# A two-layer hybrid trunk on one core: the loads of the first projection all in one queue, and five narrow products of zeros in place of three wide ones

## The chip, the core and the metric

The kernel runs on one core of a Trainium2 chip. A core has a matrix engine (TensorE, PE in the profile; its loads of stationary operands are listed apart as PEld), a vector engine (VectorE, DVE), a scalar engine (ScalarE, ACT), a general engine (GpSimd, POOL) and a sync engine (SyncE, SP). Each takes its instructions in a fixed order and waits on semaphores for the others. Transfers from device memory are issued by SP, ACT or POOL, and the same 16 DMA engines carry them all out. The metric is the device time of one execution, in microseconds (us), as the median of several.

## The reference, cut to what matters

The input x has 512 tokens of 1024 features. Two layers follow each other; each has a token mixer and a gated feed-forward network, both behind an RMS norm and added to the stream. Mixer A is attention over three dilated windows with 8 heads each, mixer B a causal pooling over 2, 4, 8 and 16 tokens. A last RMS norm ends it. All is float32.

```python
def rmsnorm(x, g):
    xf = x.astype(jnp.float32)
    y = xf * lax.rsqrt(jnp.mean(xf * xf, axis=-1, keepdims=True) + RMS_EPS)
    return (y * g.astype(jnp.float32)).astype(x.dtype)
...
for i in range(DEPTH):
    j = i // N_MIXERS
    if i % N_MIXERS == 0:
        x = x + dilated_attention_mixer(rmsnorm(x, attn_norm[j]), w_qkv[j], w_attn_out[j])
    else:
        x = x + pooling_mixer(rmsnorm(x, pool_norm[j]), w_pool_in[j], w_pool_group[j], pool_scale[j])
    x = x + swiglu_ffn(rmsnorm(x, ffn_norm[i]), w_ffn_gate_up[i], w_ffn_down[i])
return rmsnorm(x, final_norm)
```

What matters here is the very first step: the norm of x by `attn_norm`, and the first columns of its product with `w_qkv`.

## The kernel before, in words

**Layout.** The stream is kept transposed, features on the 128 partitions and the 512 tokens along the free dimension, as eight tiles X[0] to X[7] (256 KB each). A weight matrix comes in tiles of 128 by 1024.

**Precision.** A float32 value is kept as two parts, hi (rounded) and lo (what is left). `Product.add` (L234) forms, for each block k of 128 features, three matmuls that add up in one PSUM bank: L245 (hi of the weights with hi of the data), L246 (hi of the weights with lo of the data) and L248 (lo of the weights with hi of the data). The helper `split` (L77) makes the parts of a weight tile: L78 on ACT writes hi, L79 on DVE writes lo. From the second head on, most products use a scheme of seven products in place of eight (`seven`, L393).

**Weights later on.** After the start, `pump` (L165) walks a list of units: it issues a load on SP (L114 and L134 to L137) when a buffer of its ring is free, and splits a loaded unit some units ahead of its use. A ring for raw tiles has four buffers, one for split tiles five.

**The start, lines 698 to 733.** This is the code that the change touches. The norm weights of all norms come in one small tile `nrm` (24 KB), X[0] to X[7] in eight transfers, and the weights of the first four products in eight chunks `w_first[k]` (256 KB each; chunk k holds the block k of all four products). Three issuing engines share these loads:

- ACT's queue: nrm (L698), then X[0] (L700);
- POOL's queue: X[1] to X[7] (L700), then the identity `ident` (L701) and two tables of distances `d0` and `d12` (L702, L703);
- SP's queue: `w_first[0]` to `w_first[7]` (L718).

For each k the kernel then prepares the operands and adds block k to all four products at once:

- the chunk's hi on ACT (L719) and its lo on DVE (L721);
- `scaled` (L286): X[k] times the norm weight; hi on ACT (L292), for k=0 on DVE (L290), and lo on DVE (L293). The factor 1/rms, a number of each token, is multiplied in only after the product;
- `square` (L276): the squares of X[k] on ACT (L278) and their running sum on DVE (L283), from which 1/rms comes (`rstd`, L303: L309 on PE, L312 on DVE, L314 on POOL; `spread`, L317: L322 on PE).

That is twelve matmuls of 512 columns for a k, 96 for the four products. A fifth product follows (L726), the first one whose weights come by `pump` (w_qk, L114), then `rstd`, a sixth product and the rest of the first head.

**Products of zeros.** Ahead of all this, PE multiplies a tile of zeros: DVE fills `idle` (L707), and L710 runs WARM = 3 float32 products of 128 by 128 with 512 columns into a PSUM bank that nobody reads. Each such float32 product stands in the profile as two matmuls.

**What sets the order.** The program is written through a framework that inserts the semaphores and lays out the instructions of each engine by a planner with costs of its own, so that the order on an engine need not be the order of the code. DMAs of one kind share a small set of semaphores in turn; a DMA can therefore wait at its issue for an earlier one to land.

Of the kernel before, what the change touches and what calls it, by code (L numbers as in the profile page):

```python
# [8 lines left out]
F32 = mybir.dt.float32  # L9
# [7 lines left out]
P = 128  # L17
S = 512
D = 1024
KC = D // P  # L20
# [13 lines left out]
H2 = S // 2  # L34
K2 = KC // 2
NPLAIN = 6
WARM = 3
NSOLO = 3
DOWN = (6, 5)
BUFS = {"w": 5, "half": 2, "raw": 4, "rawhalf": 2}  # L40
# [8 lines left out]
def trunk(ctx: ExitStack, tc: tile.TileContext, xT, norms, w_first, w_qk, w_qkp, w_v0, w_v12, w_out, w_pair, w_down, w_pin, w_pgrp,  # L49
          dist0, dist12, ident_in, invcnt_in, outT):  # L50
    nc = tc.nc
# [6 lines left out]
    def x_tile(k, name="x", dtype=F32):  # L58
        return cpool.tile([P, S], dtype, tag=f"x{k}", name=name)

    X = [x_tile(k) for k in range(KC)]
    nrm = cpool.tile([P, NORMS, KC], F32, name="nrm")
# [4 lines left out]
    def ps():  # L67
        return psum.tile([P, S], F32, tag="ps", name="ps")
# [207 lines left out]
    def square(layer, k, engine=None):  # L276
        sq = tmp.tile([P, S], F32, name="sq")
        nc.scalar.activation(sq, X[k], AF.Square)  # L278
        if layer not in acc:
            acc[layer] = sq  # L280
            return
        new = tmp.tile([P, S], F32, name="acc")
        (engine or nc.vector).tensor_add(new, acc[layer], sq)  # L283
        acc[layer] = new

    def scaled(layer, k, hi, lo, on_dve=False):  # L286

        g = nrm[:, layer, k:k + 1]
        if on_dve:
            nc.vector.tensor_scalar(hi, X[k], g, None, op0=OP.mult)  # L290
        else:
            nc.scalar.activation(hi, X[k], AF.Copy, scale=g)  # L292
        nc.vector.scalar_tensor_tensor(lo, X[k], g, hi.bitcast(F32), op0=OP.mult, op1=OP.subtract)  # L293
        operand[layer, k] = hi, lo
# [159 lines left out]
    with tc.tile_pool(name="opool", bufs=1) as opool:  # L454
        early = opool.tile([P, HEADS, S], F32R, tag="o", name="early")
        with tc.tile_pool(name="apool", bufs=1) as apool:
# [238 lines left out]
                return apool.tile([P, S], F32, tag="scratch", name=name, bufs=3)  # L695


            nc.scalar.dma_start(nrm, norms)  # L698
            for k in range(KC):
                (nc.gpsimd if k else nc.scalar).dma_start(X[k], xT[:, k, :])  # L700
            nc.gpsimd.dma_start(ident, ident_in)  # L701
            nc.gpsimd.dma_start(d0, dist0)  # L702
            nc.gpsimd.dma_start(d12, dist12)  # L703
            lead = [Product(KC, stream(0), w=(None, None)) for i in range(NF)]

            idle = apool.tile([P, S], F32, tag="s0", name="idle")
            nc.vector.memset(idle, 0.0)  # L707
            spare = ps()
            for i in range(WARM):
                nc.tensor.matmul(spare, idle[:, :P], idle, start=True, stop=True)  # L710
            for k in range(KC):
                if k % 2 == 0:
                    rawh, wh = Held("raw"), Held("w")
                    rawh.done()
                    wh.done()
                    raw, (hi, lo) = rawh.t, wh.t
                s = slice(k % 2 * NF * P, (k % 2 + 1) * NF * P)
                nc.sync.dma_start(raw[:, s], w_first[k])  # L718
                nc.scalar.activation(hi[:, s], raw[:, s], AF.Copy)  # L719
                scaled(0, k, *U[k], on_dve=k == 0)  # L720
                nc.vector.tensor_tensor(lo[:, s], raw[:, s], hi[:, s].bitcast(F32), op=OP.subtract)  # L721
                for i, f in enumerate(lead):
                    f.w = (hi, lo)
                    f.add([k], pos=k % 2 * NF + i - k)
                square(0, k)
# [90 lines left out]
    with tc.tile_pool(name="fpool", bufs=2) as fpool:  # L816
# [217 lines left out]
        spare = {}  # L1034
# [67 lines left out]
```

## Time and profile before

| | before |
|---|---|
| median of 3 runs | 1278.92 us (1278.1 to 1279.34) |
| the profiled execution | 1279.44 us |
| its span in the trace | 1277.6 us |
| PE busy | 1262.7 us (99%), 8032 matmuls |
| DVE busy | 867.2 us (68%) |
| ACT busy | 529.7 us (41%) |
| POOL busy | 110.6 us (9%) |
| mean granted clock of TensorE | 0.995 |
| bytes moved by DMA | 163.88 MB, 128 GB/s on the mean |

How to read it: the profile is that of one execution. A row of a timeline gives start, duration, engine, line, operation, the tile written and the tiles read, with a count where several equal instructions are merged; in square brackets stands the idle time of the engine ahead of it and what ended that idle time. Matmuls overlap in a pipeline, so the distance between two starts tells more than a duration. In a table of stretches each engine has its busy time with its number of instructions in parentheses; behind them stand the granted clock of TensorE (PEclk, 1.00 is full speed), the busy share of the DMA engines and GB/s. Before the first record of the granted clock the table shows 1.00.

### The profile page before, as it was taken

What the parts mean: (1) busy time and instruction counts of PE and PEld (TensorE: products, weight loads), DVE (VectorE), ACT (ScalarE), POOL (GpSimd) and SP (SyncE); (2) the same over time, 40 slices, a digit from 0 to 9 for tenths busy, and PEclk for the clock granted to TensorE, in tenths of its full rate; (3) what the DMA queues carried; (4) which work ended last, traced back from release to release, by engine and by line L of the source; (5) the groups of instructions that cost most, each with busy time, mean ns of one, the idle gap of its engine ahead of it and who ended that gap; (6) DMA issues with size and microseconds to landing.
All of it is one profiled execution on the core that took longest, in us unless ns stands there. A gap on an engine that the chain in (4) does not pass through costs nothing.

```text
span 1277.6 us, 20114 instructions
## 1 busy us (share of the span) xinstructions
PE 1262.7 (99%) x8032; PEld 1164.0 (91%) x8032; DVE 867.2 (68%) x1313; ACT 529.7 (41%) x825; POOL 110.6 (9%) x112
## 2 busy tenths in 40 slices
PE   8999999999999999999999999999999999999997
PEld 6989999999999998889989999888788988999986
DVE  6694766568566737588736888558978953788643
ACT  6353444444334525345423554333443532455331
POOL 2101101010110100001001110000300000110000
PEclk9999999999999999999999999999999999999998
DMA  8144546445754723147446774343114645676222
GB/s 290 53 127 89 150 115 151 120 108 161 117 124 116 174 76 116 66 99 173 131 134 157 185 182 129 101 146 116 50 67 114 178 130 132 173 182 172 92 69 66
DMA packets 83006, 163.88 MB, mean 128 GB/s; under 512 B 27440, under 2 KB 29504, under 8 KB 82912
## 3 DMA queue, kind: packets, MB, share of 16 engines
q1 hardware_dynamic: 66496, 130.70, 33.0%
q0 software_dynamic: 14976, 30.55, 13.8%
q10 hardware_dynamic: 1440, 1.34, 0.3%
q8 instruction: 63, 1.03, 0.3%
q14 instruction: 31, 0.25, 0.1%
HBM read 160.40 MB, written 2.16 MB: 127 GB/s over the span
## 4 chain that ended last, share of the span: by engine, by line
PE 80%; issue 10%; DVE 6%; DMA 2%; ACT 1%; POOL 0%; DVEq 0%; SPq 0%; POOLq 0%
PE ps L385 12%; PE ps L386 12%; PE ps L384 12%; PE ps L245 9%; PE ps L246 9%; PE ps L248 9%; PE ps L484 2%; PE ps L485 2%; PE ps L486 2%; DVE wlo L79 1%; PE ps L647 1%; PE ps L510 1%; PE ps L509 1%; PE ps L511 1%; PE ps L573 1%
## 5 line engine op out<-in xcount | busy, mean ns | idle before, releaser
L79 DVE TENSOR_TENSOR wlo<-raw,whi 128x1024 fp32r<-128x1024 f32 (+2 forms) x286 | 327.2, 1147 | 203.4 <-ACT whi L78 201.8
L78 ACT ACTIVATE whi<-raw 128x1024 fp32r<-128x1024 f32 (+2 forms) x286 | 283.7, 998 | 421.7 <-PE ps L246 205.6
L245 PE MATMUL ps<-a,whi 128*128 128x512 f32 (+1 forms) x374 | 141.0, 377 | 0.0
L246 PE MATMUL ps<-a,whi 128*128 128x512 f32 (+1 forms) x374 | 140.9, 377 | 0.0
L248 PE MATMUL ps<-a,wlo 128*128 128x512 f32 (+1 forms) x374 | 140.8, 377 | 0.0
L384 PE MATMUL ps<-tt,whi 128*128 128x256 f32 x384 | 108.7, 283 | 0.0
L385 PE MATMUL ps<-tt,whi 128*128 128x256 f32 x384 | 108.7, 283 | 0.0
L386 PE MATMUL ps<-tt,wlo 128*128 128x256 f32 x384 | 108.7, 283 | 0.0
L248 PEld LDWEIGHTS ps<-a,wlo 128*128 128x128 f32 x374 | 70.4, 188 | 13.0
L246 PEld LDWEIGHTS ps<-a,whi 128*128 128x128 f32 x374 | 70.4, 188 | 12.8
L245 PEld LDWEIGHTS ps<-a,whi 128*128 128x128 f32 x374 | 70.4, 188 | 12.6
L137 POOL DMA_DIRECT2D raw<-w_pair x32 | 38.3, 1197 | 446.4 <-DMA raw<-w_pair 180.7
L384 PEld LDWEIGHTS ps<-tt,whi 128*128 128x128 f32 x384 | 73.7, 192 | 0.0
L385 PEld LDWEIGHTS ps<-tt,whi 128*128 128x128 f32 x384 | 73.7, 192 | 0.0
L386 PEld LDWEIGHTS ps<-tt,wlo 128*128 128x128 f32 x384 | 73.7, 192 | 0.0
L385 PE MATMUL ps<-tb,whi 128*128 128x256 f32 x256 | 72.5, 283 | 0.4 <-DVE tb L79 0.4
L386 PE MATMUL ps<-tb,wlo 128*128 128x256 f32 x256 | 72.4, 283 | 0.0
L384 PE MATMUL ps<-tb,whi 128*128 128x256 f32 x256 | 72.4, 283 | 0.0
L245 PE MATMUL ps<-h,whi 128*128 128x512 f32 x160 | 62.7, 392 | 0.0
L248 PE MATMUL ps<-h,wlo 128*128 128x512 f32 x160 | 62.3, 389 | 0.0
L246 PE MATMUL ps<-h,whi 128*128 128x512 f32 x160 | 62.3, 389 | 0.0
L384 PE MATMUL ps<-h,whi 128*128 128x256 f32 x216 | 61.8, 286 | 0.0
(248 smaller groups left out, 3334.1 us busy)
## 6 DMA issues: line engine op xcount, KB each, us to landing
raw<-w_pair SPq DMA_DIRECT2D x76, 512.0 KB, 4.3
raw<-w_qkp SPq DMA_DIRECT2D x36, 512.0 KB, 4.6
raw<-w_pair POOLq DMA_DIRECT2D x32, 512.0 KB, 6.9
raw<-w_v SPq DMA_DIRECT2D x24, 512.0 KB, 3.3
raw<-w_down SPq DMA_DIRECT2D x32, 384.0 KB, 3.0
raw<-w_down SPq DMA_DIRECT2D x32, 320.0 KB, 2.8
raw<-w_qkp POOLq DMA_DIRECT2D x18, 512.0 KB, 7.1
rawhalf<-w_pair SPq DMA_DIRECT2D x32, 256.0 KB, 3.3
```

What stands on the lines that cost most here:

```text
L78: nc.scalar.activation(hi, v, AF.Copy)
L79: nc.vector.tensor_tensor(lo, v, hi.bitcast(F32), op=OP.subtract)
L137: nc.gpsimd.dma_start(self.b.t.rearrange("p (a c) -> p a c", a=2), self.src[:, None, 3 * S:].to_broadcast([P, 2, S]), accum_op=OP.add)
L245: nc.tensor.matmul(self.p[:, cols], w[0][:, s], mh[:, cols], start=self.done == 0, stop=False)
L246: nc.tensor.matmul(self.p[:, cols], w[0][:, s], ml[:, cols], start=False, stop=False)
L248: nc.tensor.matmul(self.p[:, cols], w[1][:, s], mh[:, cols], start=False, stop=self.done == self.n)
L384: nc.tensor.matmul(dst, w.t[0][:, c], th, start=k == 0, stop=False)
L385: nc.tensor.matmul(dst, w.t[0][:, c], tl, start=False, stop=False)
L386: nc.tensor.matmul(dst, w.t[1][:, c], th, start=False, stop=k == K2 - 1)
L484: nc.tensor.matmul(ps4[b], oph[:, b, :], wh, start=k == 0, stop=False)
L485: nc.tensor.matmul(ps4[b], oph[:, b, :], wl, start=False, stop=False)
L486: nc.tensor.matmul(ps4[b], opl[:, b, :], wh, start=False, stop=k == KC - 1)
```

## The change

The norm weights and the eight X[k] are no longer issued by ACT and POOL. SP issues them: nrm first, and then, inside the loop over k, X[k] right before `w_first[k]`. POOL keeps `ident`, `d0` and `d12`, which are now its first transfers. The number of products of zeros goes from three to five, and each has 256 columns in place of 512; the tile of zeros is half as wide.

```diff
-WARM = 3
+WARM = 5
...
-            nc.scalar.dma_start(nrm, norms)
-            for k in range(KC):
-                (nc.gpsimd if k else nc.scalar).dma_start(X[k], xT[:, k, :])
+            nc.sync.dma_start(nrm, norms)
             nc.gpsimd.dma_start(ident, ident_in)
             nc.gpsimd.dma_start(d0, dist0)
             nc.gpsimd.dma_start(d12, dist12)
             lead = [Product(KC, stream(0), w=(None, None)) for i in range(NF)]

-            idle = apool.tile([P, S], F32, tag="s0", name="idle")
+            idle = apool.tile([P, H2], F32, tag="s0", name="idle")
             nc.vector.memset(idle, 0.0)
             spare = ps()
             for i in range(WARM):
-                nc.tensor.matmul(spare, idle[:, :P], idle, start=True, stop=True)
+                nc.tensor.matmul(spare[:, :H2], idle[:, :P], idle, start=True, stop=True)
             for k in range(KC):
...
                 s = slice(k % 2 * NF * P, (k % 2 + 1) * NF * P)
+                nc.sync.dma_start(X[k], xT[:, k, :])
                 nc.sync.dma_start(raw[:, s], w_first[k])
```

## The prediction

> **What bounds the kernel now.** I read the head of the page first, then the list of what TensorE (PE) waited for, then the first microseconds engine by engine.
>
> ```profile
> span 1277.6 us, 20114 instructions
> PE 1262.7 (99%) x8032; PEld 1164.0 (91%) x8032; DVE 867.2 (68%) x1313; ACT 529.7 (41%) x825; POOL 110.6 (9%) x112
> ```
> ```profile
> PE ps L245 <- DVE early L290: 2.5, 1, 2.5
> PE ps L710 <- DVE idle L707: 1.5, 1, 1.5
> PE ps L322 <- POOL rcol L314: 1.1, 1, 1.1
> ```
>
> PE is the bound: 99% busy, and the columns of the second list (us in total, times, longest) show that two of its largest waits lie at the very start: 1.5 us before its first product and 2.5 us before the first real one. What the change can win must come out of that start; whatever PE does earlier there, the end should follow. Here is PE's start, from its timeline (start, duration, line, count).
>
> ```profile
> 1.50 4.96 PE L710 MATMUL ps<-idle 128*128 128x512 f32 x6 [1.50 <-DVE idle L707]
> 9.01 1.85 PE L245 MATMUL ps<-early,whi 128*128 128x512 f32 x4 [2.54 <-DVE early L290]
> 10.66 0.63 PE L246 MATMUL ps<-early,whi 128*128 128x512 f32 x1
> 11.09 0.63 PE L248 MATMUL ps<-early,wlo 128*128 128x512 f32 x1
> ...
> 13.43 0.39 PE L245 MATMUL ps<-early,whi 128*128 128x512 f32 x1
> ...
> 14.12 0.39 PE L245 MATMUL ps<-early,whi 128*128 128x512 f32 x1
> ```
>
> The pitch is what counts, since durations overlap: 0.43 us (10.66 to 11.09) early, and three matmuls in 0.69 us, 0.23 us each, from 13.43 on. So PE starts its real work at 9.01 and does it at half speed for a while. The granted clock says for how long (the first pair of numbers is the stretch and its length, PEclk the third from the end):
>
> ```profile
> 9.01:9.30 0.29, 0.29 (x1) 0.26 (x2) 0.29 (x1) 0.29 (x2) 0.13 (x1) 0.86 1.03 410
> 9.30:12.50 3.20, 3.20 (x9) 2.45 (x8) 2.88 (x6) 3.20 (x7) 0.41 (x1) 0.50 1.03 386
> 12.50:12.70 0.20, 0.20 (x2) 0.19 (x1) 0.20 (x1) 0.20 (x2) 0.00 (x0) 0.67 0.92 338
> ```
>
> A mean of 0.86 over 0.29 us puts the fall to one half at about 9.22, and 0.67 over 0.20 us puts the return at about 12.63: 3.41 us at half speed, 1.7 us lost. PE thus stands as if it had begun at full speed at 9.01 + 1.7 = **10.7 us**. I call this its effective start.
>
> Why is k=0 so late? The other engines:
>
> ```profile
> 0.96 0.48 DVE L707 MEMSET idle<- 128x512 f32 x1
> 4.28 0.69 DVE L721 TENSOR_TENSOR wlo<-raw,whi 128x512 fp32r<-128x512 f32 x1 [2.83 <-ACT whi L719]
> 7.71 0.75 DVE L293 SCALAR_TENSOR_TENSOR early<-x,nrm,early 128x512 fp32r<-128x512 f32 x1 [2.73 <-ACT early L292]
> 8.38 0.48 DVE L290 TENSOR_SCALAR early<-x,nrm 128x512 fp32r<-128x512 f32 x1
> ```
> ```profile
> 0.72 0.41 ACTq L698 DMA_DIRECT2D nrm<-norms  x1
> 1.23 0.39 ACTq L700 DMA_DIRECT2D x<-xT  x1
> 3.62 0.63 ACT L719 ACTIVATE whi<-raw 128x512 fp32r<-128x512 f32 x1 [0.96 <-DMA raw<-w_first]
> 6.95 0.72 ACT L292 ACTIVATE early<-x,nrm 128x512 fp32r<-128x512 f32 x1 [2.71 <-DMA x<-xT]
> ```
> ```profile
> x<-xT ACTq DMA_DIRECT2D x1, 256.0 KB, 4.0
> ```
>
> The first weights are split by 5.0 and X[0] lands at 1.23 + 4.0 = 5.2. But L290, the only instruction of k=0 that needs X[0] first, stands on VectorE (DVE) behind an L293, which waits for L292 on ScalarE (ACT). An L293 subtracts what L290 or L292 has written; L290 writes for k=0 and comes later here, so this L293 is of k=1 and waits for X[1], which GpSimd (POOL) fetches and which is there at 6.95. The order laid out for DVE took X[1] to come before X[0]. That is 8.38 - 5.2 = 3.2 us of delay made by queues, not by data.
>
> **The change, step by step.**
>
> 1. *Warm-up.* The memset halves: 0.24 us by proportion, 0.48 if its cost is fixed, so PE starts at 1.26 to 1.50; I take 1.27, since far smaller memsets of this kernel are far shorter. The weight loads of the six warm-up matmuls give the pitch:
>
> ```profile
> 4.23 0.34 PEld L710 LDWEIGHTS ps<-idle 128*128 128x128 f32 x1 [0.52 <-issue]
> 5.08 0.34 PEld L710 LDWEIGHTS ps<-idle 128*128 128x128 f32 x1 [0.52 <-issue]
> ```
>
> That is 0.85 us for one of two matmuls of a product of 512 columns. Five products of 256 columns are ten matmuls of 0.43, 4.27 us: they end at **5.5** (5.8 by the longer memset) instead of 6.46.
>
> 2. *Arrival of k=0.* On SP stand nrm, X[0], w_first[0] in this order. The first issue is at 0.73, as now; by the ACT rows the two ahead of the weights take 0.41 and 0.39, so w_first[0] is issued at 1.53.
>
> ```profile
> 0.73 4.60 SPq L718 DMA_DIRECT2D raw<-w_first  x8
> ```
> ```profile
> DMA to landing us min/median/max: 2.9/9.9/12.3
> ```
>
> The fastest w_first, the first one, lands 2.9 us after its issue (0.73 + 2.9 = 3.6, where L719 starts). With the same delay X[0] lands at 4.0 and w_first[0] at 4.4. For the bounds: the bytes that all engines moved are 47, 234 and 389 KB in the three microseconds from 1 on; nrm, X[0] and w_first[0], 549 KB, are in by 3.7 at that rate, which is the lower bound; with the 4.0 of X[0] on ACT's queue the weights land at 5.5, the upper.
>
> ```profile
> 1.00:2.00 1.00, 0.49 (x1) 0.50 (x2) 0.45 (x1) 0.84 (x1) 0.74 (x1) 1.00 0.17 47
> 2.00:3.00 1.00, 1.00 (x2) 0.34 (x2) 0.00 (x0) 0.65 (x2) 1.00 (x3) 1.00 0.69 234
> 3.00:4.00 1.00, 1.00 (x2) 0.34 (x1) 0.00 (x0) 0.38 (x1) 1.00 (x3) 1.00 1.09 389
> ```
>
> I take 4.4, the row nearest in kind. L719 (0.63) then ends at 5.0 and L290 (0.48, from 4.0) at 4.5; L293 ends at 5.2 and L721 at 5.9, needed only after the four L245. So PE could begin at 5.0 (6.2 by the upper bound), inside or just behind the warm-up: real work starts at **5.5**, without a gap.
>
> 3. *The clock.* In the profile the grant changes at 9.22 and 12.63, 3.41 apart. One step earlier is 5.8; a rise there fits the warm-up, whose six pitches of 0.85 would end at 6.6 and not by 6.46 without it. If the steps lie so again, the real work runs at half speed from 5.5 to 5.8, 0.15 us lost: effective start **5.7**. [...]
>
> 4. *Does it stay fed?* PE eats a k in 12 x 0.23 = 2.7 us. DVE, the slower of the two that prepare it, repeats its three instructions of a k every 1.86:
>
> ```profile
> 12.93 0.74 DVE L293 SCALAR_TENSOR_TENSOR early<-x,nrm,early 128x512 fp32r<-128x512 f32 x1
> ...
> 14.79 0.75 DVE L293 SCALAR_TENSOR_TENSOR early<-x,nrm,early 128x512 fp32r<-128x512 f32 x1
> ```
>
> The DMA engines, at the 389 GB/s above, bring a pair (524 KB) in 1.35 us. POOL no longer issues X, so ident, d0 and d12 (393 KB by their shapes) come early and may push the second pair back by up to 1.0 us: it lands by 6.8 at the latest and, with L719 and L721 behind it, is ready at 8.1; PE, done with k=0 after 0.15 + 2.7, wants it at 8.4. That is close, and every later k has 0.9 us more. SP now has 17 issues in a row, 0.57 us each by the L718 row (4.60 for 8), and
>
> ```profile
> SPq L718 <- DMA nrm<-norms: 0.3, 1, 0.3
> ```
>
> shows that a ninth DMA waits for the first to land. With eight in flight, 5 us of transfer, that costs no bandwidth. Behind them on SP stands the first w_qk load, which may move by a microsecond either way. Its user is the fifth product:
>
> ```profile
> 22.64 3.49 DVE L79 TENSOR_TENSOR wlo<-raw,whi 128x1024 fp32r<-128x1024 f32 x3
> ```
>
> The first of these three splits is done at about 23.8. PE reaches it at 10.7 + 96 x 0.23 = 32.6 now and at 27.6 then, so 3.8 us of cover remain even if DVE did not move at all. Later splits wait for PE itself, and move with it.
>
> 5. *The end.* PE's last four small products run at half speed there and at full speed earlier:
>
> ```profile
> 1262.53 0.60 PE L322 MATMUL ps<-ident,rcol 128*128 128x128 f32 x4
> ...
> 1269.62 1.22 PE L322 MATMUL ps<-ident,rcol 128*128 128x128 f32 x4 [1.10 <-POOL rcol L314]
> ```
>
> Shifted against the steps of the clock they may save up to 0.6; I take 0.2.
>
> **Sum.** 10.7 - 5.7 = 5.0 us at the start, 0.2 at the end. The profiled execution took 1279.44 (span 1277.6 and 1.84 around it), 0.5 above the median: 1279.44 - 5.2 = **1274.2 us**.
>
> [...]
>
> **Rivals.**
>
> [...]
>
> *B: k=0 is still late.* DVE or ACT again has a k=1 instruction ahead of one of k=0. X[1], fourth in the queue, has its 262 KB 0.7 us after w_first[0], at 5.1, or at 5.8 beside POOL's loads; L292 (0.72), L293 (0.75) and L290 (0.48) after it end at 7.7. PE pauses 2.2 us. If the clock holds, that is the effective start and the time 1276.2; if it falls as it does now, 1.7 more, 1277.9. For it: just that inversion stands in the present order. Against: X[0] now is ahead of everything but nrm.
>
> *C: the gain is given back.* The fifth product, or a later split, doesn't come sooner and PE waits for it. From 3.8 us late on it costs one for one; 1276.5 to 1278.9. Against: the longest wait of PE after 9.01 is 1.1 us, and that for POOL.
>
> *D: slower.* One mechanism: the single queue feeds PE's first ks too slowly. Now PE begins k=7 at 10.7 + 7 x 2.7 = 29.8. With 2 us of work-up, the last pair must land after 27.8 to make the end later than it is, that is 3.3 us for each pair behind the first at 4.4: the queue would have to fall to 157 GB/s. At 4.0 us a pair PE would begin k=7 at 34.4, 4.6 later than now, and the time would be 1284. For it: the median w_first took 9.9 us to land, by the row above, if beside other queues. Against: the 389 GB/s.
>
> **Chances.** Forecast with A 66%, B 16%, C 12%, D 6%. A difference of under 0.2%, 2.6 us, can hardly be told from none; that puts the border at 1276.4. Faster: 66 + 5 of B + 3 of C = 74%; same: 11 + 9 = 20%; slower: 6%. The range begins at 1272.9 (the earliest rise, 0.6 at the end, and half of the 0.5 by which the profiled execution lies above the median) and reaches to 1277.2, with most of B and the better part of C's low end, which leaves out 20%.
>
> **What would show it.** In the changed profile: L290 ahead of every L293 on DVE, at about 4; L710 as ten matmuls ending near 5.5 to 5.8; the first L245 then, with no wait of over 0.7 us; a granted clock that has no stretch at 0.50 beginning after 9; the fifth product begun near 27.6. An L245 after 7, a half-speed stretch to 12, or new PE waits past 27 would show the forecast wrong.

## The result, and the profile after

The changed kernel takes 1275.68 us (median of 22 executions, 1274.39 to 1278.55) beside 1278.93 us before (22 executions, 1276.94 to 1280.93): a ratio of 0.9977, with an interval of 0.997 to 0.9983. It is 3 us faster; 4.7 had been forecast. The time lies within the predicted range, and the gain came from where it was looked for, the start of PE; two terms of the sum, the landing of the first weights and the rise of the clock, had the wrong size.

The profiled execution of the changed kernel took 1277.5 us, its span is 1275.7. Head of its page, and the list of what PE waited for:

```profile
span 1275.7 us, 20125 instructions
PE 1262.7 (99%) x8036; PEld 1165.3 (91%) x8036; DVE 866.3 (68%) x1313; ACT 529.4 (41%) x825; POOL 106.4 (8%) x105
```
```profile
PE ps L322 <- POOL rcol L314: 1.3, 2, 1.1
PE ps L708 <- DVE idle L705: 1.2, 1, 1.2
PE ps L309 <- ACT sq L1002: 0.8, 1, 0.8
...
PE ps L245 <- ACT whi L718: 0.5, 1, 0.5
```

The wait of 2.5 us for L290 is gone. In its place stands one of 0.5 us for L718, the hi of the first weights (line numbers of this part have moved: L708 is the product of zeros, L718 was L719, L720 was L721). PE's timeline, and then the instructions on DVE and ACT that make k=0 ready:

```profile
1.24 4.63 PE L708 MATMUL ps<-idle 128*128 128x256 f32 x10 [1.24 <-DVE idle L705]
6.41 0.79 PE L245 MATMUL ps<-early,whi 128*128 128x512 f32 x1 [0.54 <-ACT whi L718]
...
9.56 0.63 PE L246 MATMUL ps<-early,whi 128*128 128x512 f32 x1
9.99 0.55 PE L248 MATMUL ps<-early,wlo 128*128 128x512 f32 x1
10.38 0.39 PE L245 MATMUL ps<-early,whi 128*128 128x512 f32 x1
10.61 0.40 PE L246 MATMUL ps<-early,whi 128*128 128x512 f32 x1
```
```profile
4.30 0.49 DVE L290 TENSOR_SCALAR early<-x,nrm 128x512 fp32r<-128x512 f32 x1 [3.12 <-DMA x<-xT]
4.82 0.75 DVE L293 SCALAR_TENSOR_TENSOR early<-x,nrm,early 128x512 fp32r<-128x512 f32 x1
...
5.73 0.63 ACT L718 ACTIVATE whi<-raw 128x512 fp32r<-128x512 f32 x1 [0.89 <-DMA raw<-w_first]
```

Three things are to be seen. L290 now stands ahead of every L293 on DVE and runs at 4.30 in place of 8.38. The first weights land only at 5.73, so real work begins at 6.41, 0.54 us after the zeros. And its pitch is 0.43 us up to 9.99 and 0.23 us from 10.38 on: the clock rises at about 10.3 (the first record of the granted clock is at 10.31), and 3.9 us of real work ran at half speed.

With half of that lost, the effective start is 6.4 + 1.95 = 8.4 us, against 10.7 before: 2.4 us gained at the start. To see what becomes of them, I follow one instruction through both traces: L314 on POOL, which stands once in each norm. First the kernel before (start, duration), then the changed one; the rows at 39.17 and 36.81 are the first norm.

```profile
39.17 1.04 POOL L314 TENSOR_TENSOR rcol<-var,nhalf 128x4 f32<-128x4 f32 x1 [19.83 <-DVE var L312]
...
869.47 1.95 POOL L314 TENSOR_TENSOR rcol<-var,nhalf 128x4 f32<-128x4 f32 x1 [105.12 <-DVE var L312]
928.38 1.02 POOL L314 TENSOR_TENSOR rcol<-var,nhalf 128x4 f32<-128x4 f32 x1 [2.15 <-DVE var L312]
1260.36 0.71 POOL L314 TENSOR_TENSOR rcol<-var,nhalf 128x2 f32<-128x2 f32 x1 [88.41 <-DVE var L312]
```
```profile
36.81 1.04 POOL L314 TENSOR_TENSOR rcol<-var,nhalf 128x4 f32<-128x4 f32 x1 [28.75 <-DVE var L312]
...
867.41 1.95 POOL L314 TENSOR_TENSOR rcol<-var,nhalf 128x4 f32<-128x4 f32 x1 [105.53 <-DVE var L312]
926.32 1.96 POOL L314 TENSOR_TENSOR rcol<-var,nhalf 128x4 f32<-128x4 f32 x1 [2.19 <-DVE var L312]
1258.90 0.71 POOL L314 TENSOR_TENSOR rcol<-var,nhalf 128x2 f32<-128x2 f32 x1 [88.45 <-DVE var L312]
```

The lead is 2.36 us at the first norm, 2.06 at the third and fourth, and 1.46 at the last part of the kernel. The largest step down goes along with an L314 of 1.96 us where the trace before has one of 1.02. PE waits for that L314,

```profile
928.34 1.16 PE L322 MATMUL ps<-ident,rcol 128*128 128x128 f32 x8 [0.20 <-POOL rcol L314]
```

and starts this L322 1.74 us ahead of the trace before (930.08), so about 0.3 us of the 0.6 go there; the rest goes later, and its place is not shown. At the end 0.5 us come back:

```profile
1268.16 0.71 PE L322 MATMUL ps<-ident,rcol 128*128 128x128 f32 x4 [1.10 <-POOL rcol L314]
```

These are the products that took 1.22 us at half speed before. There the granted clock falls to one half at 1268.7 (a mean of 0.74 over the half microsecond from 1268.5), ahead of these products at 1269.62; here it falls at 1269.8 (0.83 over the half microsecond from 1269.5), behind them. In a second execution of the changed kernel (after_again, below) they take 1.19 us.

```profile
1265.99 1.19 PE L322 MATMUL ps<-ident,rcol 128*128 128x128 f32 x4 [1.10 <-POOL rcol L314]
```

So this pair of traces shows 1.9 us in the spans; the medians of 22 executions differ by 3.25, because the executions of one kernel differ among each other by up to 4 us, and at 1277.5 us this execution is among the longer ones of its kernel. Why they differ is the first question for the runs.

### The profile page after: what moved, and what is told of

Its sections match the earlier page's. It is cut to its first block, busy times and chain, and to the rows that moved or that the text cites. A ratio compares the mean times of both kernels' runs of the same rounds, so it can differ in the third digit from the quotient of the medians.

```text
span 1275.7 us, 20125 instructions
## 1 busy us (share of the span) xinstructions
PE 1262.7 (99%) x8036; PEld 1165.3 (91%) x8036; DVE 866.3 (68%) x1313; ACT 529.4 (41%) x825; POOL 106.4 (8%) x105
## 4 chain that ended last, share of the span: by engine, by line
PE 80%; issue 10%; DVE 6%; DMA 2%; ACT 1%; POOL 1%; SPq 0%; DVEq 0%; POOLq 0%; ACTq 0%
PE ps L385 12%; PE ps L384 12%; PE ps L386 12%; PE ps L245 9%; PE ps L248 9%; PE ps L246 9%; PE ps L484 2%; PE ps L485 2%; PE ps L486 2%; DVE wlo L79 2%; PE ps L647 1%; PE ps L510 1%; PE ps L509 1%; PE ps L511 1%; PE ps L573 1%
```

## The experiments

My theory after the result: the time is set by the effective start of PE, which is made of (1) when the operands of k=0 are ready and (2) when the clock rises, and the rise stands at no fixed distance from the start. The rivals: the zeros themselves carry the gain; the single queue as such does; the order of DVE alone does. The table gives, for each run, the median of its executions and of the kernel before on the same chip, the ratio with its interval, and from its profile PE's first real matmul and the start of the L314 of the first norm (39.17 in the profile before), which sums up the effective start. The ratio is not the quotient of the two medians but lies near that of the means (for e3 the medians alone give 0.9978). e4_tables_late, e4_again and e10_x_rows have five executions each, the changed kernel 22, the others eleven or twelve.

| run | us | before | ratio | first real | L314 |
|---|---|---|---|---|---|
| changed kernel | 1275.68 | 1278.93 | 0.9977 (0.9970 to 0.9983) | 6.41 | 36.81 |
| after_again | 1275.91 | 1278.80 | 0.9983 (0.9973 to 0.9994) | 6.35 | 35.22 |
| e1_queue_only | 1276.45 | 1279.69 | 0.9976 (0.9968 to 0.9985) | 6.96 | 35.81 |
| e2_zeros_only | 1279.09 | 1279.69 | 0.9999 (0.9990 to 1.0007) | 8.89 | 40.26 |
| e3_six | 1276.81 | 1279.69 | 0.9993 (0.9981 to 1.0005) | 7.30 | 36.07 |
| e6_eight | 1276.67 | 1278.80 | 0.9985 (0.9976 to 0.9994) | 8.01 | 36.85 |
| e8_none | 1277.67 | 1278.92 | 0.9993 (0.9984 to 1.0001) | 7.49 | 37.63 |
| e5_x0_sp | 1276.77 | 1278.80 | 0.9984 (0.9976 to 0.9993) | 7.16 | 36.15 |
| e9_two_queues | 1276.35 | 1278.80 | 0.9985 (0.9976 to 0.9994) | 6.32 | 36.06 |
| e4_tables_late | 1274.66 | 1279.69 | 0.9967 (0.9954 to 0.9980) | 5.55 | 35.76 |
| e4_again | 1274.41 | 1278.92 | 0.9968 (0.9955 to 0.9980) | 5.56 | 34.83 |
| e10_x_rows | 1274.51 | 1278.92 | 0.9965 (0.9953 to 0.9977) | 5.4 | 33.97 |

### The same kernel again

No edit.

> The changed kernel once more, unaltered, beside the other three on one chip. If the phase of the clock's steps is free, as I hold, the rise in this profile lies at another distance from the start than the 10.3 of the first one; if it is tied to the start, it is 10.3 again within 0.3. Time 1275.7 within 1, the executions spread over 3 us or more.

```profile
6.35 0.57 PE L245 MATMUL ps<-early,whi 128*128 128x512 f32 x1 [0.48 <-ACT whi L718]
6.76 0.39 PE L246 MATMUL ps<-early,whi 128*128 128x512 f32 x1
6.99 0.40 PE L245 MATMUL ps<-early,whi 128*128 128x512 f32 x1
```

Real work starts at 6.35, as in the first profile, and after the zeros the same pause stands, but the pitch is 0.23 us from 6.76 on: the clock rose at about 6.5, not 10.3. The rise is not tied to the start. L314 comes 1.6 us sooner (35.22 for 36.81) with the first real product at nearly the same time, and the execution took 1275.81 in place of 1277.5: this is most of the difference between the two executions. Spread of this set: 1274.8 to 1278.7.

The pause in itself did not hold the clock down here: it lies within the 3.41 us before this rise (the distance of the two changes of the clock in the profile before, 9.22 and 12.63), too.

```profile
3.12:6.53 3.41, 2.93 (x8) 1.83 (x7) 1.44 (x3) 1.26 (x2) 1.20 (x2) 1.00 0.92 309
```

PE was busy for 2.93 us of this stretch, and the clock rose. In the first profile it was busy for 2.88 of the 3.42 us that end at 6.90, and the pitch stayed at 0.43 us. The first profile is the exception: by the clock records of the traces, the rise comes ahead of the first real product, at 4.2 to 7.2 us, in each of the eight profiles below that have products of zeros and L290 ahead of every L293.

### The two parts of the change, each alone

e1_queue_only:

```diff
-WARM = 5
+WARM = 3
...
-            idle = apool.tile([P, H2], F32, tag="s0", name="idle")
+            idle = apool.tile([P, S], F32, tag="s0", name="idle")
...
-                nc.tensor.matmul(spare[:, :H2], idle[:, :P], idle, start=True, stop=True)
+                nc.tensor.matmul(spare, idle[:, :P], idle, start=True, stop=True)
```

> The queue part of the change alone: nrm, X and the first weights on SP as in the changed kernel, but three products of zeros of 512 columns as before. [...] Three wide products end at about 6.6, so there is no pause: PE goes on into the real products at 6.6, the clock rises by 8.3 at the latest, effective start 6.6 to 7.5 against 8.4 in the profile of the changed kernel; time 1274.8 (1273.9 to 1275.7), not slower than the whole change. Rival: the narrow products carry a part of the gain; then this is 1 us or more slower than the whole change, 1276.7 or above.

e2_zeros_only has the same lines the other way round, in the kernel before.

> The zeros part alone: the queues as before, five products of zeros of 256 columns. My theory: k=0 is still ready at about 9.0 us, the zeros end at 5.9, PE pauses 3.1 us, the clock falls or has not risen at all; effective start 10.5 to 11, time 1278.9 within 0.8, no gain. Rival: five narrow products warm the clock better than three wide ones; then 1.5 us faster, 1277.4.

The queue alone gives 0.9976, the whole of the gain (its median of 1276.45 lies above the 1273.9 to 1275.7 expected, on a chip where the kernel before takes 1279.69); the zeros alone give 0.9999. So the new zeros add nothing that these runs can see, with or without the new queue. The profile of e1 departs from its expectation in one point: its weights landed at 6.27, and PE paused after all,

```profile
6.96 0.50 PE L245 MATMUL ps<-early,whi 128*128 128x512 f32 x1 [1.02 <-ACT whi L718]
7.29 0.40 PE L246 MATMUL ps<-early,whi 128*128 128x512 f32 x1
```

but at full clock, and the clock stayed up through the pause of 1.02 us (pitch 0.23 us from 8.03 on). In e2 the other case can be seen, in an execution that was the longest of its set (1281.02). Its clock fell at 8.09, before the real work at 8.89, and this whole stretch then ran at half (PE busy 2.60 us of 3.41, clock 0.50):

```profile
8.09:11.50 3.41, 2.60 (x6) 2.15 (x7) 3.41 (x7) 3.41 (x7) 0.54 (x1) 0.50 1.04 404
```

The clock came back only at about 14.9 (pitch 0.43 us up to 14.58, 0.23 from 14.97 on). That cost its L314 1.1 us against the kernel before.

### More zeros, and none

```diff
-WARM = 5
+WARM = 6
```

> The changed kernel with six products of zeros instead of five. My theory: the zeros end at 6.4 to 6.5, the pause of 0.5 us ahead of the first real product is gone, the clock rises by 8.1 at the latest: effective start 6.5 to 7.4, time 1274.7, 1 us faster than the changed kernel. Rival: a pause of 0.5 us does not matter to the clock, the late rise at 10.3 in that profile was chance; then the time is that of the changed kernel, 1275.7, or 0.1 more.

e6_eight has WARM = 8, e8_none has WARM = 0.

> The changed kernel with eight narrow products of zeros instead of five. [...] Eight products last to 8.1 if the clock does not rise, so there is no pause before it has; effective start 6.9 to 8.1 in every execution. The executions then lie closer together (within 1.5 us, where the changed kernel spreads over 4), and the median is that of the changed kernel within 0.7. Rival: the spread of the changed kernel has nothing to do with the clock at the start; then it stays at 3 us or more, and the median is 0.5 to 1 us higher for the longer zeros.

> The changed kernel without any product of zeros. [...] Rival: the zeros buy nothing once the loads come in order; then the ratio is 0.998 as for the changed kernel.

More zeros buy nothing. Six gave 0.9993, with three of its twelve executions at 1281 to 1283; no trace of one of these was taken, and their cause stays open. Its profile, at 1275.47, shows why the reasoning of "no pause" fell: the clock rose early, at about 4.2, the twelve matmuls of zeros ended at 5.5 where the ten of the changed kernel ended at 5.87, and PE paused 1.78 us until the weights had come:

```profile
7.30 0.50 PE L245 MATMUL ps<-early,whi 128*128 128x512 f32 x1 [1.78 <-ACT whi L718]
```
```profile
4.17:7.58 3.41, 1.63 (x7) 1.13 (x7) 1.53 (x3) 1.46 (x3) 2.23 (x3) 1.00 1.01 337
```

So a number of zeros was no fixed time in these two profiles. And after the pause the clock was still up (pitch 0.23 us from 7.64 on), with 1.63 us of work in the 3.41 us shown. Eight zeros did not narrow the spread to 1.5 us (1275.3 to 1279.3), so the clock at the start is not its only source: the landing of the first weights varies too, from 5.7 to 7.3 us in the six profiles in which SP brings all of X and POOL's tables are its first transfers (the changed kernel twice, e1, e3, e6, e8).

None at all gave 0.9993, where I had expected 0.9992 (0.9985 to 1.0), an estimate with real work at half speed for 3 to 6.5 us: 1.3 to 2.0 us worse than the changed kernel by the ratios. Its interval lies just above that of the changed kernel's first set and overlaps that of after_again, so this is likely, not shown. The missing zeros are not all that the profile shows: the weights landed at 6.80 and real work began at 7.49, not at 6.41 as in the changed kernel, so a part of its late L314 is the landing and not the missing zeros. Its first matmuls, cold, and the first warm ones:

```profile
7.49 0.79 PE L245 MATMUL ps<-early,whi 128*128 128x512 f32 x1 [7.49 <-ACT whi L718]
8.08 0.63 PE L246 MATMUL ps<-early,whi 128*128 128x512 f32 x1
8.50 0.63 PE L248 MATMUL ps<-early,wlo 128*128 128x512 f32 x1
...
10.97 0.39 PE L248 MATMUL ps<-early,wlo 128*128 128x512 f32 x1
11.21 0.40 PE L245 MATMUL ps<-early,whi 128*128 128x512 f32 x1
```

The pitch is 0.43 until 10.6 and 0.23 from 10.97 on: 3.4 us ran at half speed, 1.7 us lost. It is the one trace without zeros.

### POOL's tables out of the way

```diff
             nc.sync.dma_start(nrm, norms)
-            nc.gpsimd.dma_start(ident, ident_in)
-            nc.gpsimd.dma_start(d0, dist0)
-            nc.gpsimd.dma_start(d12, dist12)
...
                 square(0, k)
+            nc.sync.dma_start(d0, dist0)
+            nc.sync.dma_start(d12, dist12)
+            nc.sync.dma_start(ident, ident_in)
             lead += begin(1, 0, range(KC))
```

> The changed kernel, but ident, d0 and d12 go through SP's queue behind the last first weight, so POOL issues none of the first transfers. My theory: POOL's three transfers are what delays w_first[0] (landed at 5.7 where 4.4 was forecast); without them it lands by 4.8, PE begins right behind the zeros at 5.9, effective start 5.9 to 7.0, time 1274.2. Rival: the low rate of 132 GB/s between 3 and 4 us has another cause (the latency of the queue's first transfers); then w_first[0] lands at 5.4 or later and the time is that of the changed kernel within 0.5.

> The run with the late tables once more, unaltered: ident, d0 and d12 on SP behind the last first weight, five narrow products of zeros. My theory: without POOL's transfers among the first ones w_first[0] lands at 4.9 in place of 5.7, PE goes on from the zeros at 5.6 without a pause, so 1 us or more is gained on the changed kernel: ratio to the kernel before 0.9972 or less. The pause of 1.06 us at k=1 in the first profile of this kernel was one DMA engine that came 2.8 us behind the other fifteen; it is chance and need not be there again. Rival: the five executions of the first time were lucky; then the ratio is that of the changed kernel, 0.998.

This is the term that the prediction had missed. The stretch from 3 to 4 us, first in the changed kernel and then in e4_again (last number: GB/s):

```profile
3.00:4.00 1.00, 1.00 (x4) 0.73 (x4) 0.00 (x0) 0.00 (x0) 0.12 (x1) 1.00 0.59 132
```
```profile
3.00:4.00 1.00, 1.00 (x4) 0.73 (x4) 0.00 (x0) 0.00 (x0) 0.00 (x0) 1.00 0.83 283
```

and what follows on ACT and PE in e4_again:

```profile
4.88 0.63 ACT L715 ACTIVATE whi<-raw 128x512 fp32r<-128x512 f32 x1
```
```profile
5.56 0.50 PE L245 MATMUL ps<-early,whi 128*128 128x512 f32 x1 [0.18 <-ACT whi L715]
5.90 0.39 PE L246 MATMUL ps<-early,whi 128*128 128x512 f32 x1
```

Without POOL's 393 KB beside them the first weights land at 4.88 in place of 5.73, real work starts at 5.56, at full clock, and 4.3 us are gained at L314. The landing differs by more in the other profiles: it is at 4.7 to 4.9 us in the three with late tables and one queue (e4 twice, and e10 below) and at 5.7 to 7.3 in the six named above. All engines together moved less in this microsecond beside POOL's transfers (132 against 283 GB/s), so it is more than the sharing of one rate; why is open. This kernel is very likely also the faster one: 0.9967 and 0.9968 on two chips, 1.2 to 2.0 us below the changed kernel by the ratios (0.9983 and 0.9977 less 0.9968 and 0.9967, of 1279). The two intervals overlap in part with those of the changed kernel, so it is the two agreeing repeats, and e10 with 0.9965, together with the rows above that carry this. In the first profile of this kernel PE paused 1.06 us at k=1, where w_first[1] landed at 8.9; the records of landing show that fifteen of its sixteen shares had come by 6.1 and the last at 8.9. In the second it landed at 7.2.

### Order or queue?

e5_x0_sp moves one transfer of the kernel before:

```diff
-            for k in range(KC):
-                (nc.gpsimd if k else nc.scalar).dma_start(X[k], xT[:, k, :])
+            nc.sync.dma_start(X[0], xT[:, 0, :])
+            for k in range(1, KC):
+                nc.gpsimd.dma_start(X[k], xT[:, k, :])
```

> The kernel before with one transfer moved: X[0] goes out on SP ahead of w_first[0]; nrm stays on ACT, X[1] to X[7] and the tables on POOL, three wide products of zeros. DVE's order laid out for it has L290 first. My theory: most of the gain of the change is that the instruction of k=0 no longer stands behind one of k=1. L290 then runs at about 4.2 and w_first[0] lands at about 5; PE starts its real work at 6.6, right behind the zeros, and waits again for k=1 (X[1] by POOL lands at 6.9, so the second k is ready at about 8.5, no long pause). Effective start 6.8 to 8, time 2.5 us or more below the kernel before: ratio 0.998 or less. Rival: the single queue is what counts, because X[1] to X[7] on POOL hold up the first ks; then the gain is under 1 us, ratio over 0.999.

e9_two_queues is e4 with two words changed:

```diff
-            nc.sync.dma_start(nrm, norms)
+            nc.scalar.dma_start(nrm, norms)
...
-                nc.sync.dma_start(X[k], xT[:, k, :])
+                nc.scalar.dma_start(X[k], xT[:, k, :])
```

> As the run with the late tables (ident, d0, d12 on SP behind the last first weight), but nrm and all X go out on ACT's queue and only w_first on SP. Five narrow products of zeros. The order laid out for DVE has two L717 and L290 ahead of the first L293. My theory: two queues shared by the same DMA engines bring X[k] and w_first[k] side by side, so a pair arrives as with one queue, no later than 5.7; what counted in the change is that POOL does not bring X. PE starts at 5.6 to 6.2, time as with the late tables on one queue, 1274.7 within 0.7. Rival: one queue in the order of need is what counts; on two queues the loads of later ks run ahead of those of k=0, PE starts at 7 or later and the time is 1 us or more above that.

In e5 only X[0] has moved, DVE's order has turned, and L290 runs at 4.17:

```profile
4.17 0.49 DVE L290 TENSOR_SCALAR early<-x,nrm 128x512 fp32r<-128x512 f32 x1 [2.72 <-DMA nrm<-norms]
```

The ratio, 0.9984, lies within the interval of the changed kernel on the same chip (0.9983). So the bulk of the gain comes with moving X[0]; taking X[1] to X[7] off POOL adds less than these runs can tell apart. The move does two things, since X[0] also lands sooner (4.0 in place of 5.2), and a run with the order alone turned was not made. By the rows of the kernel before, an L290 run at 5.2 would have ended at 5.7, ahead of the end of the zeros at 6.46, so the order by itself could account for the wait of 2.5 us; that is an estimate.

On ACT the inversion came back: the first weights, issued at 1.16, landed 3.5 us later (4.7), but their hi stands behind the L292 of k=1.

```profile
5.87 0.72 ACT L292 ACTIVATE early<-x,nrm 128x512 fp32r<-128x512 f32 x1 [1.24 <-DMA x<-xT]
6.50 1.13 ACT L720 ACTIVATE whi<-raw 128x512 fp32r<-128x512 f32 x2
```
```profile
7.16 0.50 PE L245 MATMUL ps<-early,whi 128*128 128x512 f32 x1 [1.34 <-ACT whi L720]
```

So e5 pays for a k=1 instruction ahead of one of k=0 as well, only less.

For e9 my theory fell and the rival held. The two queues are served side by side, w_first[0] lands at 3.56, but X[0] only at 5.7:

```profile
5.68 0.49 DVE L290 TENSOR_SCALAR early<-x,nrm 128x512 fp32r<-128x512 f32 x1 [0.77 <-DMA x<-xT]
```

and PE starts at 6.32, 0.8 us later than with one queue; the time is 0.9985 against 0.9967 and 0.9968 (on other chips). With the tables gone, one queue in the order of need gives about 2 us over two queues by these ratios. DVE's order turned too (an L717 ran at 4.23, ahead of this L290), but it was done at 4.92 and the row names the transfer as what L290 waited for; the ratios are of different chips and their intervals overlap a little, so the 0.8 us at the start is the firmer number. Not all of the 2 us need be the sharing of two queues: ACT also computes, and it issued X[1] only at 3.57, behind an L715,

```profile
3.57 0.34 ACTq L713 DMA_DIRECT2D x<-xT  x1
```

where SP issues it at 2.1 in e4. A second queue on an engine that does not compute was not tried.

### How x lies in memory

e10_x_rows is e4 with x stored as eight contiguous blocks, so that X[k] is read as one (a later load of x, on POOL, is changed in the same way):

```diff
-                nc.sync.dma_start(X[k], xT[:, k, :])
+                nc.sync.dma_start(X[k], xT[k])
...
-        "xT": v["x"].reshape(S, KC, P).transpose(2, 1, 0),
+        "xT": v["x"].reshape(S, KC, P).transpose(1, 2, 0),
```

> As the run with the late tables, but x lies in device memory so that each X[k] is one contiguous block of 256 KB, as each w_first[k] is, in place of 128 rows 16 KB apart. The order of all instructions is the same. Theory: it makes no difference, since the rows of 2 KB are the same transfers; X[0] lands at 4.2 and the time is that of the late tables within 0.7. Rival: the low rate of the first microseconds (132 GB/s between 3 and 4 us in the changed kernel, 285 with the late tables) comes from the stride of x; then X[0] and w_first[0] land 0.5 us sooner or more.

```profile
3.76 0.49 DVE L290 TENSOR_SCALAR early<-x,nrm 128x512 fp32r<-128x512 f32 x1 [2.58 <-DMA x<-xT]
```
```profile
4.72 0.63 ACT L715 ACTIVATE whi<-raw 128x512 fp32r<-128x512 f32 x1 [0.42 <-DMA raw<-w_first]
```

X[0] lands 0.5 us sooner than in e4 (L290 at 3.76 in place of 4.30), the weights 0.15 sooner, and PE has no pause in the first ks. The rival was right on X[0], not on the weights, and the time, 0.9965, cannot be told from e4's.

## Why the prediction was right, and where its sizes were off

**What bounds the kernel**: right. PE's start was the place, and what was won there reached the last norm but for 0.9 us of 2.36 in this pair of traces.

**Step 1, the zeros**: 4.27 us from 1.27 were forecast, ending at 5.5; the last of the ten matmuls ends at 5.87 in the profile, with its tail, from a start at 1.24. Right.

**Step 2, arrival of k=0**: the step that failed. L290 ahead of every L293, with X[0] at 4.0 forecast and 4.2 measured, was right. The landing of w_first[0] was put at 4.4, at the most at 5.5; it was 5.7, beyond the bound. The transfers of ident, d0 and d12 were seen, but step 4 had them start after k=0 was in and push back the second pair. They hit the first: POOL issues them at 1.3 to 3.1 now that nothing stands ahead of them on POOL, while the seven X kept them until 5.2 before. e4 measures the term: 0.85 us of the 1.3 at the landing. The other half microsecond is there without the tables too: in e4_again w_first[0] is issued at 1.63, not 1.53, and lands 3.2 us later (4.88), where the forecast gave the third transfer of a queue the 2.9 us that the first one had taken.

**Step 3, the clock**: the rise 3.41 us before 9.22 was carried over as if tied to the start, with an effective start of 5.7. It is not tied: the clock rose at 10.3 and 6.5 in two profiles of one kernel. The effective start was 8.4 in the first: of the 2.7 us beyond the forecast 0.9 are the later real start, the rest the later rise. The 3.42 us that end 3.41 us before that rise, at 6.9, have a pause of 0.54 us in them; those before the rise in after_again have one of 0.48 us, so a pause alone doesn't explain it. PE was busy for 2.88 us of the one and 2.93 of the other; what decides between them was not shown. No run shows an earliest or a latest rise either, as the range (its "earliest rise"), rival A (8.1) and the expectations of e1, e3 and e6 (8.3 and 8.1) took it: those were estimates of mine, and the rise came at 10.3, at 6.5 and, in e3, at 4.2. With rises this far apart in one kernel, a mean over several profiles would have served the forecast better than the one of the profile before.

Chance has a part in the number 1274.2. e4_again has nearly what the forecast assumed, the landing at 4.9, a pause of 0.18 us and an early rise; by L314 it starts effectively at 10.7 - 4.3 = 6.4, not 5.7, and its profiled execution took 1274.2, the very number forecast, because its lead grew from 4.3 us at the first norm to 5.1 at the last, for reasons not looked into.

**Step 4, fed afterwards**: right. PE's waits after 6.41 are those of before within 0.2 us (the longest, for L314, is again 1.1), and the fifth product moved along with the start, from 32.5 to 30.1 where 27.6 was forecast.

**Step 5, the end**: 0.2 was taken of a bound of 0.6; the profile had 0.5, after_again next to nothing (1.19 against 1.22). It goes by when the clock falls there, at 1268.7 in the profile before and at 1269.8 in the first of the changed kernel.

**The rivals**: A, a rise at 8.1 and a time of 1275.3, is in kind what the first profile shows, with a rise at 10.3. B and D did not occur (D's 29.8 is 29.6 by its own terms, which changes nothing). C, a gain given back, is a part of the first pair of traces: 0.3 us up to the third norm and 0.6 from the fourth on, beside an L314 that took 0.9 us longer. That L314 takes about 2.0 us in every profile with L290 ahead of every L293 (1.96 in both of the changed kernel) and 1.0 us in the two without (the kernel before, 1.02, and e2); what makes it so wasn't tried.

## What to carry to other kernels

When an engine waits at the start, look at what its feeder was made to wait for: here a transfer that had landed at 5.2 was used at 8.38, because the laid-out order put an instruction of the next step ahead of it, and moving one transfer (e5) gave most of the gain. A transfer that is taken off a queue lets the ones behind it start sooner, and here they delayed the most urgent ones; move the tables that nobody needs yet behind them (e4: very likely one to two microseconds more). A gain of a few microseconds at the start must be judged over many executions, since the rise of the clock alone moved the start by 1.6 us between two of them.

## What the runs showed of the hardware

- **When the clock changed.** In the profile before, the granted clock stands at full speed from its first record at 5.81, at one half from 9.22 and at full speed again from 12.63, 3.41 us apart each time. In the 3.41 us that end at its rise PE was busy for 2.93 us in after_again (above) and, within 0.01 us, in e3. With PE busy for 2.60 of 3.41 us (e2, from 8.09 on) it stayed at one half, and so it did in the changed kernel with 2.88 of the 3.42 us that end at 6.90:

```profile
3.48:6.90 3.42, 2.88 (x7) 1.84 (x6) 1.75 (x3) 1.26 (x2) 1.41 (x2) 1.00 0.93 335
```

  (PEclk reads 1.00 there since no record of the clock exists yet; the pitch of 0.43 up to 9.99 tells the clock.) At full clock it stayed up with PE busy for 1.63 of 3.41 us (e3, from 4.17 on), and it fell after 0.87 us in the kernel before:

```profile
5.82:9.23 3.41, 0.87 (x3) 0.26 (x2) 1.52 (x3) 1.73 (x3) 0.60 (x2) 1.00 1.01 361
```

  What decides this was not shown. A pause of 0.54 us at half clock was followed by half speed up to 10.3 in the changed kernel, one of 0.48 us by a rise at 6.5 in after_again, and after one of 1.78 us at full clock the pitch was 0.23 us (e3).
- **The last of sixteen shares counts.** In the changed kernel the sixteen shares of w_first[0] landed from 5.07 to 5.71 us, and L718, which waits for it, ran at 5.73. In the first profile of e4 the last share of a transfer of 256 KB came up to 2.8 us behind the fifteenth; with x in contiguous blocks (e10) the first six transfers had all shares within 0.6 us. These are single profiles; which engine lags, and why, is open.
- **One queue and two.** With X and the weights on two queues (e9) w_first[0] came at 3.6 and X[0] at 5.7; on one queue (e4) at 4.9 and 4.2. The pair is complete 0.8 us sooner in one queue, in one profile of e9 and two of e4.
